# The low part of W1's chunks in the MLP loop: made by ScalarE and an accumulating GpSimd transfer instead of VectorE

## Chip, cores, metric

The kernel runs on one core of a Trainium2 chip. The metric is device time in microseconds (us) of one execution; a time is the median of several executions. Engines go by their short names in the rows: PE (TensorE, matmuls), PEld (its weight loads), DVE (VectorE), ACT (ScalarE), POOL (GpSimd), SP (SyncE, which issues the loads here).

## What is computed

One decoder layer on x of 256 tokens by 1024 in float32: a mixer of four column groups, and an MLP of width 4096. The change touches the MLP alone:

```python
for l in range(DEPTH):                      # DEPTH = 1
    h = rms_norm(x, pre_mix_g[l])
    u = h @ w_in[l]
    ...
    y = jnp.concatenate([y_a, y_b, y_c, y_d], axis=-1) @ w_out[l]
    x = x + rms_norm(y, post_mix_g[l])
    h = rms_norm(x, pre_mlp_g[l])
    m = jnp.square(jax.nn.relu(h @ mlp_w1[l])) @ mlp_w2[l]
    x = x + rms_norm(m, post_mlp_g[l])
```

## The kernel before

**Three products for one.** To keep float32 accuracy every large product is split. A weight chunk arrives as `raw` (128 partitions by 2048, 1 MB). ScalarE copies it to a tile `hi` of type fp32r (`split_hi`), VectorE writes `lo = raw - hi` (`split_lo`). The activations are split in the same way (`h2`, `h2L`; `mh`, `ml`). TensorE then runs three matmuls for each product: hi by hi, hi by activation lo, and lo by hi.

**The chunks.** `seq` (lines 87 to 92) lists all weight chunks in the order of use: 10 of W_in, 4 of W_out, then for the MLP `w1 0, w1 1, w2 0, w1 2, w2 1, w1 3, ...`, 16 of W1 and 16 of W2. Tiles come from the pool `wts`: four buffers each for `raw` and `hi`, three for `lo`, handed out in turn. So the `lo` of a chunk takes the buffer of the chunk that came three splits before it, and a `raw` that of the chunk four loads before it.

**The MLP loop** (lines 887 to 898) walks `seq` from n = 14. At a W1 chunk c it issues `up(c)`: 48 matmuls of 256 columns into a PSUM tile `pm`, in groups of three whose third reads `lo`. At a W2 chunk c it issues `down(c)`: 30 matmuls into the sums `acd` that stay in PSUM. After either, it issues the load of the chunk four places on (SP), the split of the chunk two places on, and after `up(c)` the squared ReLU and its split (`relu2`, `act`). Each engine works through its own instructions strictly in the program's order (`InOrder`), so PE runs up(1), down(0), up(2), down(1), up(3), ... without choice, and ACT runs for each c: relu of up(c), `mh` of c, `hi` of W2's chunk c, `hi` of W1's chunk c + 2. W1's chunks 0 and 1 are split ahead of the loop; the loop itself splits W1's chunks 2 to 15 and all of W2.

**The end.** `down(14)` and `down(15)` are ordered so that the first 128 tokens finish early; `finish` scales, adds the residual and stores the output in five pieces (SP). After that, lines 957 to 964 run 20 matmuls into a PSUM tile `shapes` which nothing reads.

In the profile all instructions carry the line of the helper (L60), so they are told apart by the names of their tiles: `hi_w`, `lo_w`, `raw_w` are the tiles of W1 and W2 alike.

Of the kernel before, what the change touches and what calls it, by code (L numbers as in the profile page):

```python
# [16 lines left out]
F32 = mybir.dt.float32  # L17
F32R = mybir.dt.float32r
BF16 = mybir.dt.bfloat16
AF = mybir.ActivationFunctionType  # L20
ALU = mybir.AluOpType
# [3 lines left out]
P = 128  # L25
# [3 lines left out]
NW = 2048  # L29
# [36 lines left out]
def hybrid_layer(ctx, tc, x, head, win, wout, w1, w2, gates, rows, out):  # L66
    nc = tc.nc
    V, A, G, T, Q = (InOrder(tc, e) for e in (nc.vector, nc.scalar, nc.gpsimd, nc.tensor, nc.sync))

    cst = ctx.enter_context(tc.tile_pool(name="cst", bufs=1))  # L70
    wts = ctx.enter_context(tc.tile_pool(name="wts", bufs=4))
# [11 lines left out]
    def mm(name):  # L83
        return pmm.tile([P, 512], F32, tag="mm", name=name)


    seq = [("in", c) for c in (0, 1, 8, 5, 6, 7, 9, 3, 4, 2)]
# [5 lines left out]
    src = {"in": win, "out": wout, "w1": w1, "w2": w2}  # L93
    raw, hi, lo = {}, {}, {}
# [6 lines left out]
    def load(n, parts=1):  # L101
        if n < len(seq):
            w, d = new_raw(n)
            for i in range(parts):
                c = slice(i * NW // parts, (i + 1) * NW // parts)
                Q.dma_start(w[:, c], d[:, c])
# [4 lines left out]
    def split_hi(n, i=0, parts=1):  # L111
        if n < len(seq):
            k = seq[n]
            if i == 0:
                hi[k] = wts.tile([P, NW], F32R, tag="hi", name=f"hi_{k[0]}{k[1]}")
            c = part(i, parts)
            A.activation(hi[k][:, c], raw[k][:, c], AF.Copy)

    def split_lo(n, i=0, parts=1):
        if n < len(seq):  # L120
            k = seq[n]
            if i == 0:
                lo[k] = wts.tile([P, NW], F32R, tag="lo", name=f"lo_{k[0]}{k[1]}", bufs=3)
            c = part(i, parts)
            V.tensor_tensor(lo[k][:, c], raw[k][:, c], hi[k][:, c].bitcast(F32), op=ALU.subtract)

    def split(n, parts=1):
        for i in range(parts):
            split_hi(n, i, parts)
            split_lo(n, i, parts)  # L130
# [6 lines left out]
    for blocks in HEAD:  # L137
        n = HOFF[blocks[-1]] + S
# [16 lines left out]
    warm = cst.tile([P, 256], BF16, name="warm")  # L155
# [117 lines left out]
    identb = cst.tile([P, P], BF16, name="identb")  # L273
# [568 lines left out]
    def up(c, between=None):  # L842
        pu = mm(f"pm{c}")
        H, L = hi["w1", c], lo["w1", c]
        for j in range(2):
            if j and between:
                between()
            o = pu[:, j * S:(j + 1) * S]
            for k in range(KT):
                ws = slice(k * S + j * P, k * S + (j + 1) * P)  # L850
                T.matmul(o, H[:, ws], h2[:, k, :], start=(k == 0), stop=False)
                T.matmul(o, H[:, ws], h2L[:, k, :], start=False, stop=False)
                T.matmul(o, L[:, ws], h2[:, k, :], start=False, stop=(k == KT - 1))
        return pu

    def relu2(pu):
        m = wk.tile([P, 512], F32, name="mr")
        A.activation(m, pu, AF.Relu)
        V.tensor_tensor(m, m, m, op=ALU.mult)
        return m  # L860

    def act(c, m):
        mh[c] = wk.tile([P, 512], F32R, name="mh", bufs=3)
        ml[c] = wk.tile([P, 512], F32R, name="ml", bufs=3)
        A.activation(mh[c], m, AF.Copy)
        V.tensor_tensor(ml[c], m, mh[c].bitcast(F32), op=ALU.subtract)

    m0 = relu2(pz[0])

    def act0():  # L870
# [12 lines left out]
    def down(c, t, h):  # L883
        wide("w2", c, lambda k, t: mh[c][:, k * S + t * P:k * S + (t + 1) * P],
             lambda k, t: ml[c][:, k * S + t * P:k * S + (t + 1) * P], t, accs[t, h], cols[t, h], c == 0, c == 15)

    for n in range(14, len(seq)):
        name, c = seq[n]
        if name == "w1":
            pm_ = up(c, act0 if c == 1 else None) if c else None  # L890
        elif c < 14:
            for t, h in sorted(cols):
                down(c, t, h)
        load(n + 4)
        split(n + 2)
        if pm_ is not None:
            act(c, relu2(pm_))
            pm_ = None
        if n == 14:

            for t in range(2):
                scr = few.tile([P, D], BF16, name="scr", bufs=1)
                ss = few.tile([P, 1], F32, name="ss")
                A.activation(scr, x1[t], AF.Square, accum_out=ss)
                V.tensor_scalar(q2[t], ss, 1.0 / D, RMS_EPS, op0=ALU.mult, op1=ALU.add)
                V.reciprocal(q2[t], q2[t])
# [47 lines left out]
    finish(1, ((0, 384), (384, 768), (768, 1024)))  # L954


    pb = mm("shapes")
    H15 = hi["w2", 15]
    wide_zeros = warm[:, None, :].to_broadcast([P, 2, 256])
    for lhs, rhs, n in ((H15[:, :P], H15[:, 512:1024], 512), (identb, wide_zeros, 512), (H15[:, :P], H15[:, 512:896], 384),  # L960
                        (H15[:, :P], H15[:, 512:576], 64)):
        for _ in range(5):
            T.matmul(pb[:, :n] if rhs is not wide_zeros else pb.rearrange("p (a b) -> p a b", a=2), lhs, rhs,
                     start=True, stop=True)


# [41 lines left out]
```

## Time and profile before

| | us |
|---|---|
| median of 3 runs (287.37 to 287.67) | 287.59 |
| the profiled execution | 288.29 |
| its span in the profile | 286.6 |
| PE busy / DVE / ACT / POOL | 279.3 / 193.6 / 152.6 / 22.3 |
| mean granted TensorE clock | 1.00 of full speed |

The profiled execution is 0.70 us above the median, and 1.69 us of it lie outside the span. Times inside the span are counted from its start. The MLP loop's PE work begins at 107.71 us with up(1) and is over at 279.60 us.

### The profile page before, as it was taken

The numbers are of one execution on the slowest core, as the hardware profiler recorded it, in microseconds if no ns is written. First come the engines' busy times: TensorE is split into PE (matmuls) and PEld (weight loads), VectorE is DVE, ScalarE is ACT, GpSimd is POOL, SyncE is SP. The second block draws the span as 40 slices with busy tenths as digits, with TensorE's granted clock in tenths as the row PEclk, the third lists the DMA queues.
The fourth block names the chain that finished last, engine by engine and source line by source line (L and its number), as shares of the span: only waits on it lengthen the run. The fifth ranks groups of instructions, "written<-read, shape, count | busy, mean of one in ns | idle before, by whom it ended". The sixth has DMA issues, their size and how long they took to land.

```text
span 286.6 us, 4726 instructions
## 1 busy us (share of the span) xinstructions
PE 279.3 (97%) x1954; PEld 255.9 (89%) x1954; DVE 193.6 (68%) x262; ACT 152.6 (53%) x192; POOL 22.3 (8%) x53
## 2 busy tenths in 40 slices
PE   6799999999999999999999999999999999999995
PEld 4699997999977899989999899899899899899883
DVE  1999999899989996765636646546447357257262
ACT  3995459875548849642632623624615515526141
POOL 4388500000000000000000000000000000000000
PEclk9999999999999999999999999999999999999999
DMA  6999446926404544675374383472472562600012
GB/s 210 412 409 334 150 156 225 411 74 238 146 2 153 213 150 173 266 287 214 101 281 166 129 293 133 165 293 96 199 287 74 226 255 69 266 0 0 2 73 74
DMA packets 9237, 53.04 MB, mean 185 GB/s; under 512 B 1024, under 2 KB 1536, under 8 KB 3712
## 3 DMA queue, kind: packets, MB, share of 16 engines
q1 hardware_dynamic: 9216, 52.75, 49.1%
q8 instruction: 15, 0.25, 0.3%
q14 instruction: 6, 0.05, 0.1%
HBM read 51.70 MB, written 1.05 MB: 184 GB/s over the span
## 4 chain that ended last, share of the span: by engine, by line
PE 94%; DMA 2%; DVE 1%; SPq 0%; ACT 0%; issue 0%
PE acd L60 31%; PE pm L60 29%; PE pu L60 19%; PE acc L60 7%; DMA hd<-in_head_dram 2%; PE pz L60 2%; PE shapes L60 1%; PE psc L60 1%; PE po L60 1%; DVE sq L60 1%; PE pg L60 1%; PE pth L60 0%; PE ptp L60 0%; SPq L60 0%; PE pvar L60 0%; DVE hF L60 0%
## 5 line engine op out<-in xcount | busy, mean ns | idle before, releaser
L60 DVE TENSOR_TENSOR lo_w<-raw_w,hi_w 128x2048 fp32r<-128x2048 f32 (+2 forms) x36 | 72.6, 2050 | 17.8 <-ACT hi_w L60 17.8
L60 PE MATMUL pm<-h2L,hi_w 128*128 128x256 f32 x240 | 66.5, 277 | 0.0
L60 PE MATMUL pm<-h2T,hi_w 128*128 128x256 f32 x240 | 66.5, 277 | 0.0
L60 PE MATMUL pm<-h2T,lo_w 128*128 128x256 f32 x240 | 66.4, 277 | 0.0
L60 ACT ACTIVATE hi_w<-raw_w 128x2048 fp32r<-128x2048 f32 (+1 forms) x33 | 59.6, 1849 | 1.3 <-issue 1.3
L60 PE MATMUL acd<-hi_w,ml 128*128 128x512 f32 (+1 forms) x160 | 56.0, 350 | 0.0
L60 PE MATMUL acd<-lo_w,mh 128*128 128x512 f32 (+1 forms) x160 | 55.8, 349 | 0.0
L60 PE MATMUL acd<-hi_w,mh 128*128 128x512 f32 (+1 forms) x160 | 55.8, 348 | 0.0
L60 ACT ACTIVATE mr<-pm 128x512 f32<-128x512 f32 x15 | 8.9, 596 | 73.8 <-PE pm L60 73.8
L60 PEld LDWEIGHTS pm<-h2T,hi_w 128*128 128x128 f32 x240 | 45.1, 188 | 0.0
L60 PEld LDWEIGHTS pm<-h2T,lo_w 128*128 128x128 f32 x240 | 45.1, 188 | 0.0
L60 PEld LDWEIGHTS pm<-h2L,hi_w 128*128 128x128 f32 x240 | 45.1, 188 | 0.0
L60 DVE TENSOR_TENSOR mr<-mr 128x512 f32<-128x512 f32 x16 | 11.1, 693 | 44.7 <-ACT mr L60 44.7
L60 PE MATMUL pu<-hT,hi_in 128*128 128x256 f32 x128 | 36.3, 284 | 0.0
L60 PE MATMUL pu<-hT,lo_in 128*128 128x256 f32 x128 | 35.9, 280 | 0.0
L60 PE MATMUL pu<-hL,hi_in 128*128 128x256 f32 x128 | 35.9, 280 | 0.0
L60 PEld LDWEIGHTS acd<-lo_w,mh 128*128 128x128 f32 x160 | 30.2, 189 | 4.2
L60 PEld LDWEIGHTS acd<-hi_w,ml 128*128 128x128 f32 x160 | 30.1, 188 | 4.2
L60 PEld LDWEIGHTS acd<-hi_w,mh 128*128 128x128 f32 x160 | 30.1, 188 | 4.1
L60 DVE SCALAR_TENSOR_TENSOR cacc<-zpad,prm,cacc 128x256 f32<-128x256 f32 x60 | 25.3, 477 | 0.1
L60 PEld LDWEIGHTS pu<-hT,hi_in 128*128 128x128 f32 x128 | 24.3, 190 | 0.0
L60 PEld LDWEIGHTS pu<-hT,lo_in 128*128 128x128 f32 x128 | 24.2, 189 | 0.0
(177 smaller groups left out, 381.3 us busy)
## 6 DMA issues: line engine op xcount, KB each, us to landing
raw_w<-in_w_dram SPq DMA_DIRECT2D x32, 1024.0 KB, 4.9
raw_in<-in_win_dram SPq DMA_DIRECT2D x7, 1024.0 KB, 5.6
raw_out<-in_wout_dram SPq DMA_DIRECT2D x4, 1024.0 KB, 4.9
raw_in<-in_win_dram SPq DMA_DIRECT2D x4, 512.0 KB, 7.9
hd<-in_head_dram SPq DMA_DIRECT2D x3, 384.0 KB, 5.9
x<-in_x_dram SPq DMA_DIRECT2D x2, 512.0 KB, 7.5
grow<-in_rows_dram SPq DMA_DIRECT2D x2, 512.0 KB, 7.1
hd<-in_head_dram SPq DMA_DIRECT2D x2, 256.0 KB, 4.9
```

The lines of the kernel that those rows point to most:

```text
L60: ins = f(*args, **kwargs)
```

## The change

For W1's chunks 2 to 15 the loop no longer calls `split` but `split_dma`: ScalarE writes `hi` as before, then a second ScalarE instruction writes `-hi` to the `lo` tile, and GpSimd issues a transfer that reads the chunk from HBM once more and adds it to what stands in the `lo` tile. W2's chunks are split as before. The 20 matmuls into `shapes` are gone.

```diff
+    def split_dma(n):
+
+        k = seq[n]
+        split_hi(n)
+        lo[k] = wts.tile([P, NW], F32R, tag="lo", name=f"lo_{k[0]}{k[1]}", bufs=3)
+        A.activation(lo[k], hi[k].bitcast(F32), AF.Copy, scale=-1.0)
+        G.dma_start(lo[k], src[k[0]][k[1]], accum_op=ALU.add)
...
-        split(n + 2)
+        if n + 2 < len(seq) and seq[n + 2][0] == "w1":
+            split_dma(n + 2)
+        else:
+            split(n + 2)
...
-    pb = mm("shapes")
-    H15 = hi["w2", 15]
-    wide_zeros = warm[:, None, :].to_broadcast([P, 2, 256])
-    for lhs, rhs, n in ((H15[:, :P], H15[:, 512:1024], 512), (identb, wide_zeros, 512), (H15[:, :P], H15[:, 512:896], 384),
-                        (H15[:, :P], H15[:, 512:576], 64)):
-        for _ in range(5):
-            T.matmul(pb[:, :n] if rhs is not wide_zeros else pb.rearrange("p (a b) -> p a b", a=2), lhs, rhs,
-                     start=True, stop=True)
```

What it moves on the engines shows best at the start of the loop. First ACT, from the first split inside the loop on: `hi_w_1393` is the `hi` of W1's chunk 2 and `lo_w_1395` its `lo`, `mr` and `mh` belong to the squared ReLU of up(1), and the last two `hi_w` are W2's chunk 1 and W1's chunk 3.

```order
 L60 ACTIVATE mh<-ptm 128x512
 L60 ACTIVATE hi_w_1393<-raw_w_1301 128x2048
+L60 ACTIVATE lo_w_1395<-hi_w_1393 128x2048
 L60 ACTIVATE mr<-pm_1332 128x512
 L60 ACTIVATE mh<-mr 128x512
-L60 ACTIVATE hi_w_1436<-raw_w_1316 128x2048
-L60 ACTIVATE hi_w_1491<-raw_w_1391 128x2048
-L60 ACTIVATE mr<-pm_1440 128x512
```

One ACT instruction of a whole chunk has come in ahead of the squared ReLU of up(1), and one stands at the same place in each later turn of the loop. Next DVE at the same place: `lo_w_1438` is W2's chunk 1 and `lo_w_1493` W1's chunk 3.

```order
 L60 TENSOR_TENSOR ml<-ptm,mh 128x512
-L60 TENSOR_TENSOR lo_w_1395<-raw_w_1301,hi_w_1393 128x2048
 L60 TENSOR_TENSOR mr<-mr 128x512
 L60 TENSOR_TENSOR ml<-mr,mh 128x512
-L60 TENSOR_TENSOR lo_w_1438<-raw_w_1316,hi_w_1436 128x2048
-L60 TENSOR_TENSOR lo_w_1493<-raw_w_1391,hi_w_1491 128x2048
+L60 TENSOR_TENSOR lo_w_1439<-raw_w_1316,hi_w_1437 128x2048
```

DVE loses the subtraction of every W1 chunk from 2 on and keeps those of W2 (the same tile is 1438 in one build and 1439 in the other). Last GpSimd, whose instructions ended before with the four `alibi` tiles of the mixer:

```order
 L60 TENSOR_SCALAR alibi<-dist 128x256 x4
-L1004 UNCONDITIONAL_BRANCH
-L1004 ISA
+L60 DMA lo_w_1395<-in_w_dram 128x2048
+L60 DMA lo_w_1494<-in_w_dram 128x2048
+L60 DMA lo_w_1593<-in_w_dram 128x2048
```

Fourteen such transfers follow one another there; nothing else is added to this engine.

## Rows read from the trace of the kernel before

**Rows 1.** The page, parts 1 and 2: busy time; the span in 40 slices, tenths.

```profile
PE 279.3 (97%) x1954; PEld 255.9 (89%) x1954; DVE 193.6 (68%) x262; ACT 152.6 (53%) x192; POOL 22.3 (8%) x53
...
PE   6799999999999999999999999999999999999995
...
PEclk9999999999999999999999999999999999999999
```

**Rows 2.** The page, part 4: shares of the chain that ended last, by engine.

```profile
PE 94%; DMA 2%; DVE 1%; SPq 0%; ACT 0%; issue 0%
```

**Rows 3.** That chain in order of time: start us, us, what.

```profile
107.71 2.83 PE pm L60 x24
...
113.72 5.59 PE acd L60 x30
119.31 5.45 PE pm L60 x48
124.76 5.59 PE acd L60 x30
...
207.68 5.45 PE pm L60 x48
213.13 5.59 PE acd L60 x30
218.73 5.46 PE pm L60 x48
...
279.60 3.61 PE shapes L60 x20
```

**Rows 4.** ACT in order of time, start of the loop: start, us, instructions.

```profile
112.80 1.91 ACT L60 ACTIVATE hi_w<-raw_w 128x2048 fp32r<-128x2048 f32 x1
114.60 0.58 ACT L60 ACTIVATE mr<-pm 128x512 f32<-128x512 f32 x1
117.67 0.63 ACT L60 ACTIVATE mh<-mr 128x512 fp32r<-128x512 f32 x1 [2.48 <-DVE mr L60]
118.20 3.71 ACT L60 ACTIVATE hi_w<-raw_w 128x2048 fp32r<-128x2048 f32 x2
```

**Rows 5.** PE in order of time, first lo product of up(2).

```profile
119.14 0.28 PE L60 MATMUL pm<-h2T,hi_w 128*128 128x256 f32 x1
...
119.38 0.28 PE L60 MATMUL pm<-h2T,lo_w 128*128 128x256 f32 x1
```

**Rows 6.** ACT in order of time, one later turn of the loop.

```profile
204.08 3.70 ACT L60 ACTIVATE hi_w<-raw_w 128x2048 fp32r<-128x2048 f32 x2
```

**Rows 7.** DVE in order of time, the same turn.

```profile
206.01 4.49 DVE L60 TENSOR_TENSOR lo_w<-raw_w,hi_w 128x2048 fp32r<-128x2048 f32 x2 [1.11 <-ACT hi_w L60]
```

**Rows 8.** SP in order of time, the first load that turn frees.

```profile
208.33 13.57 SPq L60 DMA_DIRECT2D raw_w<-in_w_dram  x4
```

**Rows 9.** Stretches of that turn: busy of each engine, clock, DMA share, GB/s.

```profile
204.00:209.00 5.00, 5.00 (x35) 4.59 (x34) 3.68 (x3) 3.79 (x3) 0.00 (x0) 1.00 0.00 0
209.00:215.00 6.00, 6.00 (x46) 5.65 (x45) 2.20 (x2) 1.01 (x2) 0.00 (x0) 1.00 0.91 345
215.00:216.00 1.00, 1.00 (x6) 0.78 (x6) 0.69 (x1) 1.00 (x2) 0.00 (x0) 1.00 0.08 33
```

**Rows 10.** Issues and landings of W1's and W2's loads.

```profile
DMA to landing us min/median/max: 4.7/4.9/6.5
```

**Rows 11.** Groups of instructions from 130 to 260 us, DVE and ACT chunk instructions.

```profile
L60 DVE TENSOR_TENSOR lo_w<-raw_w,hi_w 128x2048 fp32r<-128x2048 f32 x24 | 53.9, 2288 | 13.3 <-ACT hi_w L60 13.3
...
L60 ACT ACTIVATE hi_w<-raw_w 128x2048 fp32r<-128x2048 f32 x24 | 44.5, 1900 | 0.0
```

**Rows 12.** SP in order of time, the last output stores.

```profile
281.53 1.35 SPq L60 DMA_DIRECT2D out_dram<-u  x3
```

**Rows 13.** DMA issues: KB each, median us to landing (the last output piece).

```profile
out_dram<-u SPq DMA_DIRECT2D x1, 128.0 KB, 2.9
```

**Rows 14.** Waits, SP: us in total, times, longest (the program's end).

```profile
SPq L1004 <- PEq L1004: 1.0, 2, 0.8
```

## Prediction

> **What bounds the kernel now.** I read the page first: PE is busy 97% of the span, its slices stand at nine tenths from the third to the last but one, and the granted clock is at its upper level (2.4 GHz) in all of them [rows 1]. The chain that ended last is 94% PE [rows 2]. In order of time it has no piece of another engine in the MLP loop: down(0) starts at 113.72, up(2) at 119.31 when it ends, down(1) at 124.76, and a late turn (207.68, 213.13, 218.73) has the same spacing; a turn of up and down takes 5.45 + 5.59 = 11.04 us [rows 3]. So VectorE and ScalarE work there for nothing but being in time, and what the change does to the end is decided by one question: is the low part of a W1 chunk ready when its up() begins? For that I read when ScalarE finishes `hi` [rows 4, 6], when PE first reads a `lo` [rows 5], and what the DMA engines do in between [rows 8 to 10].
>
> **What goes.** Fourteen subtractions of 2.29 us [rows 11], 32 us of VectorE. None lies on the chain, so they are worth 0. The 20 unread matmuls take 3.61 us from 279.60 and end at 283.21 [rows 3], but the output's last store is issued between 281.53 and 282.88 [rows 12] and takes 2.9 us to land [rows 13], until 285.4 or so; they are covered by it: 0. At most it is the 0.8 us that SP's longest wait for PE in the closing lines took [rows 14]; the other end is 0, and I take 0, because the store outlasts them by 2 us.
>
> **What comes on ScalarE.** Fourteen more passes over a chunk. Two passes in a row take 3.71 us [rows 4], so one more is 1.80. A turn's ScalarE work is about 0.58 + 0.63 + 3.70 us [rows 4, 6] and becomes 6.7 of 11.04: 0. At the loop's start the pass delays the relu of up(1) from 114.60 to about 116.4, but in the kernel before `mh` there waited 2.48 us for VectorE's square, until 117.67 [rows 4], and the subtraction ahead of that square is gone; `mh` stays near its place: 0.
>
> **The accumulating transfer.** No row shows one. Call D the time from the end of ScalarE's `-hi` to the chunk's landing.
> - *Lower bound:* a plain 1 MB load, 4.9 us from issue to landing, 4.7 to 6.5 [rows 10].
> - *What a plain load consists of:* in a turn the DMA engines are idle from 204 to 209, then share 0.91 over six microseconds and 0.08 over one [rows 9]: 6 x 0.91 + 0.08 = 5.54 us for two chunks, so 2.77 us of moving for 1 MB. The remaining 4.9 - 2.77 = 2.13 us is the way in and out.
> - *My value:* an add needs both operands, the chunk from HBM and the 1 MB that already stands in `lo`: two chunks' reading, 5.54 us. For GpSimd's part I add its mean instruction, 22.3 us over 53 = 0.42 us [rows 1]. D alone = 0.42 + 2.13 + 5.54 = 8.1 us.
> - *Upper bound:* the nearest row for a slower adder is none; I take four chunks' moving, 0.42 + 2.13 + 11.1 = 13.6.
>
> The Trainium skill (Collectives: The Full Stack, The bandwidth ceiling: the fold count and why AG ≠ RS ≠ AR) says that a transfer that adds is not slowed by the arithmetic but by reading two sources, and gives a ratio of 1.93 against a copy. By it the moving would be 2.77 x 1.93 = 5.3 us, an estimate; by the row alone, read as a price for one chunk whatever is done with it, 2.77. No run here shows such a transfer.
>
> **The first one, W1's chunk 2.** ScalarE starts its `hi` at 112.80; two passes later `-hi` is there, 112.80 + 3.71 = 116.51 [rows 4]. PE reads the first `lo` of up(2) at 119.38, only two matmuls after up(2) began [rows 5]. The cover is 2.87 us. The loads that ran with it are a single chunk in flight at most, so D alone holds: PE waits 8.1 - 2.9 = **5.2 us**. By the lower bound it is 4.9 - 2.9 = 2.0, by the upper 10.7. Behind the waiting matmul is all of PE's queue, and every other engine waits for PE. This stall is inside the program order and can't be worked around.
>
> **The second, chunk 3.** ScalarE is not held by PE yet: its two `hi` begin at 118.20 [rows 4], and with `-hi` it is done at 118.20 + 3.71 + 1.80 = 123.7. up(3) started at 124.76 + 5.59 = 130.35 [rows 3] and now comes 5.2 later: cover 11.8, more than any D below. 0.
>
> **The turns after that, chunks 4 to 15.** `-hi` needs a `lo` buffer, which is free only when down(c - 1) has ended, 207.68 in the turn I read; ScalarE's two `hi` end at 204.08 + 3.70 = 207.78 [rows 6], `-hi` at 209.58. up(c + 2) begins at 218.73 [rows 3] and reads `lo` 0.07 later: cover 9.2 us. D alone, 8.1, would fit. But the same moment frees two `raw` buffers: W2's when VectorE's first subtraction of the turn ends (206.01 and 4.49 for two, so 208.3 [rows 7]), and SP issues at 208.33 [rows 8]; W1's now already with ScalarE's `hi` at 207.78, so its load no longer waits for a second subtraction and follows at once. GpSimd issues at 209.58 + 0.42 = 210.0, 1.67 us behind them, with 5.54 - 1.67 = 3.9 us of their moving still to do. Served ahead of the loads it lands after 8.1 us (no stall), behind them after 8.1 + 3.9 = 12.0 (stall 2.8). I take packet against packet, the adding one counting two: two thirds of the engines' time, 5.54 x 1.5 = 8.31, D = 0.42 + 2.13 + 8.31 = 10.9, a stall of 10.9 - 9.2 = 1.65 us in each turn. A stall moves everything alike, so it comes again next turn. Chunks 4 to 14 meet two loads (the last three loads fall to chunks 13 and 14), chunk 15 none: 11 x 1.65 = **18.0 us**, bounds 0 and 11 x 2.8 = 31.
>
> **Sum.** 5.2 + 0 + 18.0 = 23.2 on the profiled execution's 288.29 us: 311.5. That execution stood 0.70 above the median of the runs, so against the median 287.59 I forecast **310.8 us**.
>
> **The rivals.**
> 1. *Only the first stall remains*: the transfer wins against the loads, or costs little more than a plain one. For it: D alone fits under 9.2, and the DMA engines are idle more than half of a turn [rows 9]. Against: the loads are issued 1.67 us earlier. 287.6 + 2.0 to 5.2 = 289.7 to 292.8.
> 2. *The adder is slower than two reads.* With three chunks' moving, 8.31: alone D = 10.9, first stall 8.0; beside loads three quarters of the time, 11.1, D = 13.6, stall 4.4 in 11 turns = 48.5, and 1.7 for chunk 15. Sum 58, 346 us; with four chunks' about 382. Nothing in the trace speaks for or against.
> 3. *The clock falls.* PE has no long wait in this trace, and the clock never left 2.4 GHz [rows 1]; a wait of 5 us is new. At 1.2 GHz up(2) alone would take 5.45 more: 316. The Trainium skill (TensorE: Matmul & The Clock Gate, HAM oscillation — how this bites in real kernels) says that waits for transfers between groups of matmuls can put the array back to half its clock, and that it then starts cold. No stretch of this trace shows it.
> 4. *Not slower.* It needs the first chunk landed within 2.87 us of `-hi`, and every later one within 9.2. Then PE never waits, the time is 287.6, or 286.8 with the 0.8 us of the closing wait. For it there is only that a transfer's own moving can be 2.77 us; against it, that no 1 MB load in the loop landed in under 4.7 [rows 10]. That the change doesn't do what it says is not at issue: each listed transfer is there on GpSimd.
>
> **How the numbers follow.** Forecast 0.36, only the first stall 0.27, slower adder 0.24, clock 0.08, not slower 0.05. The forecast's own range, by the share that the loads take, is 287.6 + 5.2 = 292.8 to 287.6 + 5.2 + 31 = 323.8. For 8 in 10 I leave out not slower (0.05) and the upper half of the slower adder (0.12): 289.7 to 346. A measurement of this kernel can tell about 0.2% (0.6 us) from no change. Slower by more than that are all cases but the last: 0.95; of the last I give 0.03 to within 0.2% and 0.02 to faster.
>
> **What would show it.** In the profile after: 14 adding transfers whose landing can be read; a wait of PE for `lo_w` before up(2) of about 5 us, none before up(3), then some 1.6 us before each up() to chunk 14 and none at chunk 15; up and down otherwise 5.45 and 5.59; VectorE's `lo_w` 14 fewer; the end from the last `acd` to the span's end unchanged. Wrong would be: no wait at up(2) (rival 4), waits at up(2) alone (rival 1), waits of 4 us and more in each turn (rival 2), or up() itself longer at a granted clock under 1.00 (rival 3).

## The result and the profile after

The changed kernel takes **312.76 us** (median of 4 runs, 312.05 to 315.59) against 287.60 for the kernel before on the same chip: ratio 1.0895, 95% interval 1.0824 to 1.0965. The forecast was 310.8 us, with a range of 289.7 to 346. The execution that was profiled is the longest of the four, 315.59 us with a span of 313.9; the span has grown by 27.3 us where the median has grown by 25.2. In two of the experiments below (4 and 7) the profile is of an execution that the comparisons leave out, so only a single place is read from it.

The page of the changed kernel, parts 1 to 3, answers to [rows 1]: PE is down to 90% of the span, its slices dip all through the loop, and the granted clock has dips too. DMA share has risen to nearly ten tenths there; the new queue q0 carries GpSimd's transfers.

```profile
PE 282.6 (90%) x1934; PEld 257.6 (82%) x1934; DVE 162.7 (52%) x248; ACT 179.6 (57%) x206; POOL 34.6 (11%) x67
...
PE   6899999999999991899799699889978999799992
...
PEclk9999999999999996699899999979999999999998
DMA  7997539363053589919987996994998989957003
...
q0 software_dynamic: 2016, 14.68, 23.4%
```

VectorE's busy time fell by 193.6 - 162.7 = 31 us and bought nothing, as foreseen. The waits view of the changed kernel (who waits for whom, us in total, times, longest) names what PE had never waited for before:

```profile
PEld pm L60 <- DMA lo_w<-in_w_dram: 23.8, 10, 8.6
PE pm L60 <- DMA lo_w<-in_w_dram: 21.8, 9, 8.4
```

In order of time these are PE's first matmuls on a landed `lo` (start, us, instruction, idle time before it and its releaser). The chunks are 2, 4, 6, 8, 10, 11, 12, 13 and 14; chunks 3, 5 and 9 have no wait, chunk 7 one of 0.2 us that only PE's weight loads show, chunk 15 none:

```profile
126.93 0.58 PE L60 MATMUL pm<-h2T,lo_w 128*128 128x256 f32 x1 [8.42 <-DMA lo_w<-in_w_dram]
153.15 0.39 PE L60 MATMUL pm<-h2T,lo_w 128*128 128x256 f32 x1 [2.11 <-DMA lo_w<-in_w_dram]
179.86 0.38 PE L60 MATMUL pm<-h2T,lo_w 128*128 128x256 f32 x1 [2.71 <-DMA lo_w<-in_w_dram]
204.88 0.39 PE L60 MATMUL pm<-h2T,lo_w 128*128 128x256 f32 x1 [2.40 <-DMA lo_w<-in_w_dram]
230.86 0.39 PE L60 MATMUL pm<-h2T,lo_w 128*128 128x256 f32 x1 [1.96 <-DMA lo_w<-in_w_dram]
243.41 0.38 PE L60 MATMUL pm<-h2T,lo_w 128*128 128x256 f32 x1 [1.22 <-DMA lo_w<-in_w_dram]
255.26 0.38 PE L60 MATMUL pm<-h2T,lo_w 128*128 128x256 f32 x1 [0.53 <-DMA lo_w<-in_w_dram]
268.37 0.39 PE L60 MATMUL pm<-h2T,lo_w 128*128 128x256 f32 x1 [1.78 <-DMA lo_w<-in_w_dram]
280.40 0.39 PE L60 MATMUL pm<-h2T,lo_w 128*128 128x256 f32 x1 [0.70 <-DMA lo_w<-in_w_dram]
```

The first is 8.4 us, the others add up to 13.4. The transfers themselves, issues with KB each and median us to landing, then all landings of `lo_w`, then three of GpSimd's issues in order of time (the first, that of chunk 4, and the last, of chunk 15):

```profile
raw_w<-in_w_dram SPq DMA_DIRECT2D x32, 1024.0 KB, 6.1
lo_w<-in_w_dram POOLq DMA_DIRECT2D x14, 1024.0 KB, 11.6
...
DMA to landing us min/median/max: 7.9/11.6/13.2
...
115.94 1.04 POOL L60 DMA_DIRECT2D lo_w<-in_w_dram  x1 [83.28 <-ACT lo_w L60]
142.05 0.86 POOL L60 DMA_DIRECT2D lo_w<-in_w_dram  x1 [17.84 <-ACT lo_w L60]
281.74 0.86 POOL L60 DMA_DIRECT2D lo_w<-in_w_dram  x1 [12.24 <-ACT lo_w L60]
```

The reader should see two things. The last transfer, the only one without a load beside it, is the one that lands in 7.9 us; the median is 11.6. And from the issue of chunk 4 to that of chunk 15 there are 11 turns in 139.7 us, 12.7 each against 11.04 [rows 3].

The clock is the third item. Stretches of the changed kernel (columns as in [rows 9]: PE busy with its matmuls, PEld, DVE, ACT, POOL, granted clock, DMA share, GB/s), around the waits before up(2), up(4) and up(6), and after that before up(8):

```profile
120.00:122.00 2.00, 0.00 (x0) 0.00 (x0) 1.62 (x1) 1.97 (x2) 0.00 (x0) 0.61 1.02 205
122.00:126.00 4.00, 0.00 (x0) 0.00 (x0) 0.00 (x0) 1.03 (x1) 0.87 (x1) 0.50 0.99 295
126.00:130.00 4.00, 3.07 (x14) 3.07 (x15) 0.00 (x0) 0.00 (x0) 0.00 (x0) 0.50 1.02 320
130.00:132.00 2.00, 2.00 (x17) 2.00 (x16) 0.00 (x0) 0.00 (x0) 0.00 (x0) 0.83 0.96 262
151.00:153.00 2.00, 0.04 (x1) 0.00 (x0) 0.38 (x1) 1.79 (x1) 0.00 (x0) 1.00 0.88 188
153.00:156.00 3.00, 2.85 (x19) 2.85 (x20) 0.00 (x0) 0.00 (x0) 0.86 (x1) 0.76 0.99 374
156.00:158.00 2.00, 2.00 (x11) 2.00 (x11) 0.00 (x0) 0.00 (x0) 0.00 (x0) 0.50 1.06 324
...
178.00:180.00 2.00, 0.14 (x1) 0.14 (x2) 0.00 (x0) 0.90 (x1) 0.81 (x1) 1.00 0.84 246
180.00:182.00 2.00, 2.00 (x18) 2.00 (x19) 0.00 (x0) 0.00 (x0) 0.05 (x1) 1.00 1.04 381
...
206.00:209.00 3.00, 3.00 (x16) 3.00 (x15) 0.00 (x0) 0.00 (x0) 0.00 (x0) 0.50 1.04 344
```

The clock is at half (1.2 GHz) for the rest of the first wait and the first 3.6 us of up(2), once more after the wait before up(4), not after that before up(6), and again at up(8).

**Where the 27.3 us are.** The chain of the changed kernel, in order of time, ends its loop with `down(14)` and `down(15)`; the two lines before that show up() after a wait and at full clock, and up(2) at half clock:

```profile
126.93 7.26 PE pm L60 x46
...
280.40 5.51 PE pm L60 x46
...
296.95 11.23 PE acd L60 x60
```

From up(2)'s first matmul to the last `acd` PE took 308.18 - 118.11 = 190.1 us, before it took 279.60 - 119.14 = 160.5 [rows 3, 5]: 29.6 more. The listed waits are 8.4 + 13.4 = 21.8 of it. The half clock costs 7.26 - 5.51 = 1.75 us in up(2), and about 1.6 each in up(4) and up(8), which take 7.0 us from the end of the wait to the first matmul of down() where up(14) takes 5.34; 5.0 in all. The other 2.8 are the ends of the ten waits, 0.27 or so each: a wait is counted from the modelled end of the matmul before it, 0.28 us after its start, while matmuls that follow each other start 0.12 apart, and the first matmul after a wait holds the next one up by another 0.1. Against these 29.6 stand 1.0 us by which up(2) comes earlier than before (118.11 against 119.14, in code that the change does not touch) and 1.3 us of a shorter end, whose last store lands in 1.9 us instead of 2.9 [rows 13]. The missing matmuls don't account for the shorter end: in experiment 1, which leaves out only them, the store takes 2.9 us and the end 7.0, as before.

The two shortest of the four executions (312.05 and 312.14 us) have a mean clock of 0.987 and 0.985 and are 3.5 us shorter than the profiled one, about what its two later falls cost (3.3). That those two executions had only the first fall is likely, but no profile of them shows it.

### The profile page after: what moved, and what is told of

The parts are those of the page before. It is cut to its first block, busy times and chain, and to the rows that moved or that the text cites. A ratio compares the mean times of both kernels' runs of the same rounds, so it can differ in the third digit from the quotient of the medians.

```text
span 313.9 us, 4692 instructions
## 1 busy us (share of the span) xinstructions
PE 282.6 (90%) x1934; PEld 257.6 (82%) x1934; DVE 162.7 (52%) x248; ACT 179.6 (57%) x206; POOL 34.6 (11%) x67
## 4 chain that ended last, share of the span: by engine, by line
issue 41%; PE 41%; DMA 9%; POOL 3%; ACT 2%; DVE 2%; SPq 0%; DVEq 0%; POOLq 0%; ACTq 0%
PE pu L60 17%; DMA lo_w<-in_w_dram 7%; PE acc L60 7%; PE pm L60 6%; PE acd L60 5%; POOL lo_w L60 3%; DMA hd<-in_head_dram 2%; PE pz L60 2%; ACT hi_w L60 1%; PE psc L60 1%; PE po L60 1%; DVE sq L60 1%; ACT lo_w L60 1%; PE pg L60 1%; DVE u L60 0%
## 5 line engine op out<-in xcount | busy, mean ns | idle before, releaser
L60 PE MATMUL pm<-h2T,lo_w 128*128 128x256 f32 x240 | 69.9, 291 | 21.8 <-DMA lo_w<-in_w_dram 21.8
L60 PE MATMUL pm<-h2T,hi_w 128*128 128x256 f32 x240 | 68.7, 286 | 0.0
L60 PE MATMUL pm<-h2L,hi_w 128*128 128x256 f32 x240 | 68.6, 286 | 0.0
L60 PEld LDWEIGHTS pm<-h2T,lo_w 128*128 128x128 f32 x240 | 47.4, 197 | 23.8 <-DMA lo_w<-in_w_dram 23.8
L60 DVE TENSOR_TENSOR mr<-mr 128x512 f32<-128x512 f32 x16 | 11.1, 694 | 106.2 <-ACT mr L60 106.2
L60 DVE TENSOR_TENSOR lo_w<-raw_w,hi_w 128x2048 fp32r<-128x2048 f32 (+2 forms) x22 | 41.7, 1902 | 16.7 <-ACT hi_w L60 16.7
L60 PEld LDWEIGHTS pm<-h2T,hi_w 128*128 128x128 f32 x240 | 47.5, 198 | 0.0
L60 PEld LDWEIGHTS pm<-h2L,hi_w 128*128 128x128 f32 x240 | 47.4, 197 | 0.0
L60 POOL DMA_DIRECT2D lo_w<-in_w_dram x14 | 12.3, 875 | 237.7 <-ACT lo_w L60 237.7
L60 ACT ACTIVATE lo_w<-hi_w 128x2048 fp32r<-128x2048 f32 x14 | 26.8, 1914 | 0.4
## 6 DMA issues: line engine op xcount, KB each, us to landing
lo_w<-in_w_dram POOLq DMA_DIRECT2D x14, 1024.0 KB, 11.6
```

Of the source, the lines that this page charges most:

```text
L60: ins = f(*args, **kwargs)
```

## The experiments

The kernel before had a median of 287.74 us beside these runs. Ratios are against it.

**1. Only the unread matmuls gone.** The kernel before without lines 957 to 964.

```diff
-    pb = mm("shapes")
...
-            T.matmul(pb[:, :n] if rhs is not wide_zeros else pb.rearrange("p (a b) -> p a b", a=2), lhs, rhs,
-                     start=True, stop=True)
```

> The kernel before without its 20 unread matmuls, and nothing else of the change. Theory: they lie beside the last output store, so the time stays at 287.6 within 0.3. Rival: the closing wait of SP for PE (0.8 us in the kernel before) is theirs, and the time falls to about 286.8.

287.67 us against 287.74; ratio 0.9989, interval 0.9969 to 1.0008. Nothing that can be told from no change. That part of the change is worth 0 as far as this can tell; the rival's 0.8 us is just inside the interval's lower end (0.9 us), but the medians differ by 0.1, and the profile speaks against it: SP's longest closing wait for PE is 0.8 us there too, without the matmuls.

**2. Does the add make the transfer long, or GpSimd's issue?** The same 14 transfers as plain copies.

```diff
-        G.dma_start(lo[k], src[k[0]][k[1]], accum_op=ALU.add)
+        G.dma_start(lo[k], src[k[0]][k[1]])
```

> The changed kernel with the same 14 GpSimd transfers as plain copies, without the add; the low part then holds the whole chunk, so the second product of W1 is not the one that is wanted. Theory (the add moves two chunks' bytes): moving 2.8 us less alone and 5.5 beside the loads, landing 5 us after issue alone and 7 to 8 beside loads, under the cover of 9.2, so no waits in later turns and 3 to 5.5 us before up(2); 290 to 295. Rival (it is GpSimd's way of issuing that is slow, not the add): landings stay at 11 us and the time at 312.

294.70 us; ratio 1.0238 (1.0203 to 1.0272). In its profile PE's matmuls wait once, before up(2), and nowhere else in the loop; only its weight loads wait 0.3 us more in a later turn (PE in order of time, then the issues and the landings of `lo_w`):

```profile
124.33 0.58 PE L60 MATMUL pm<-h2T,lo_w 128*128 128x256 f32 x1 [5.10 <-DMA lo_w<-in_w_dram]
...
lo_w<-in_w_dram POOLq DMA_DIRECT2D x14, 1024.0 KB, 7.7
...
DMA to landing us min/median/max: 5.1/7.7/9.1
```

Alone (the shortest, again the last) a plain copy lands in 5.1 us and an adding one in 7.9. The difference, 2.8 us, is one more chunk's moving, 2.77 by [rows 9]. The stretches of these two lone transfers show it directly: the adding one keeps the DMA engines at a share of 0.83 for 7 us (283 to 290 us of the changed kernel), 5.8 us of moving, and the plain one at 0.58 for 5 us (263 to 268 us here), 2.9. So the add occupies the engines twice as long, and the issue by GpSimd is not what is slow: 5.1 against 4.9 for SP's loads [rows 10]. The moving goes from 2.77 to 2.77 + 2.8 = 5.57 us, a ratio of 2.0. The Trainium skill's ratio between a step that adds and one that copies, which it measured in collectives (Collectives: The Full Stack, The bandwidth ceiling: the fold count and why AG ≠ RS ≠ AR), is 1.93; the trace agrees.

**3. Half the transfers.** Odd chunks split by VectorE, even ones as changed.

```diff
-        if n + 2 < len(seq) and seq[n + 2][0] == "w1":
+        if n + 2 < len(seq) and seq[n + 2][0] == "w1" and seq[n + 2][1] % 2 == 0:
```

> The changed kernel with only W1's even chunks (2, 4, ... 14) by the adding transfer, the odd ones by VectorE: half the transfers. Theory (PE's wait before one up() is cover for the next chunk, so two neighbours share one deficit of about 2.1 to 2.7 us): waits of 1.8 to 2.7 us before up(4), up(6) ... up(14), 11 to 16 in all, about as much as the changed kernel's 13.4 with twice the transfers; wait before up(2) as there; time 309 to 313. Rival (every transfer costs alike, 13.4 over 12, 1.1 us): 6 x 1.1 = 6.7 us, time 304 to 306.

316.34 us; ratio 1.1001 (1.0967 to 1.1035): half the transfers, and no less time; it is 3 us above the theory's 309 to 313. PE's waits in its profile (chunks 2, 4, ... 14):

```profile
127.94 0.58 PE L60 MATMUL pm<-h2T,lo_w 128*128 128x256 f32 x1 [8.70 <-DMA lo_w<-in_w_dram]
154.38 0.38 PE L60 MATMUL pm<-h2T,lo_w 128*128 128x256 f32 x1 [1.87 <-DMA lo_w<-in_w_dram]
179.33 0.39 PE L60 MATMUL pm<-h2T,lo_w 128*128 128x256 f32 x1 [2.58 <-DMA lo_w<-in_w_dram]
206.06 0.39 PE L60 MATMUL pm<-h2T,lo_w 128*128 128x256 f32 x1 [2.75 <-DMA lo_w<-in_w_dram]
230.62 0.38 PE L60 MATMUL pm<-h2T,lo_w 128*128 128x256 f32 x1 [1.99 <-DMA lo_w<-in_w_dram]
256.27 0.39 PE L60 MATMUL pm<-h2T,lo_w 128*128 128x256 f32 x1 [1.66 <-DMA lo_w<-in_w_dram]
281.04 0.39 PE L60 MATMUL pm<-h2T,lo_w 128*128 128x256 f32 x1 [2.40 <-DMA lo_w<-in_w_dram]
```

The six later ones add up to 13.25 us, where the changed kernel's later ones add up to 13.4 with twice as many transfers. That settles the rule: `-hi` of chunk c + 2 is written when down(c - 1) ends, and what PE then waits before up(c + 1) is cover for chunk c + 2 as well. Two neighbours share one deficit, landing plus issue less 9.2 us; it doesn't come in each turn. That this kernel's median is even above the changed one's is the clock's doing as far as the profiles tell. The two profiled executions differ by only 0.8 us (316.40 and 315.59), with 22.0 and 21.8 us of waits. But this kernel's mean granted clock was 0.971 to 0.972 in all four runs, the changed kernel's 0.969, 0.975, 0.985 and 0.987, the lower the longer.

**4. The first transfer one chunk later.** Chunk 2 by VectorE, chunk 3 the first adding one.

```diff
-        if n + 2 < len(seq) and seq[n + 2][0] == "w1":
+        if n + 2 < len(seq) and seq[n + 2][0] == "w1" and seq[n + 2][1] > 2:
```

> The changed kernel with W1's chunk 2 split by VectorE again, so that chunk 3 has the first adding transfer. Theory (a stall is D less the cover, and the cover counts what PE waits in between): the wait of 8.4 us before up(2) goes, but chunk 3 loses the 8.4 us that it had on top of its own cover of 6.7, so with D of 11 to 11.6 PE waits 4.3 to 4.9 us before up(3); later turns as in the changed kernel; time some 4 to 6 below it, 307 to 309. Rival (the 8.4 us is a price of the first transfer as such, GpSimd after a long rest): PE waits 8 us and more before up(3), time unchanged at about 313. Second rival (the wait belongs to chunk 2 alone): no wait before up(3), about 302.5.

Ratio 1.0710 (1.0656 to 1.0764), about 308 us (two executions, 306.7 and 309.3). Of its profile only the wait before up(3) is read: 5.7 us, 0.8 above the range of the theory. The miss is the landing: 12.0 us after the issue, where the theory had 11 to 11.6 in all; 12.0 + 0.3 - 6.7 is 5.6. Both rivals fall: it is neither 8.4 again nor nothing. The wait follows the cover of the chunk that happens to be first.

**5. The loads behind the add.** GpSimd issues the loop's loads itself, after the adding transfer of the turn; only the first two (18 and 19 of `seq`) stay with SP.

```diff
-        load(n + 4)
...
+        if n == 14:
+            load(18)
+            load(19)
+        elif name == "w1":
+            load(n + 5, eng=G)
+            load(n + 6, eng=G)
```

(`load` takes the engine as an argument; the two `load` calls of a turn stand after the split.)

> The changed kernel with the loop's loads from the chunk 20 of the sequence on issued by GpSimd behind the adding transfer of the same turn, instead of by SP ahead of it; same bytes, same 14 adds. Theory (the later turns' waits are the time that the loads take ahead of the add): the add lands about 8 us after issue, as the last one did alone (7.9), under the cover of 9.2, so no waits in later turns beyond 0.3; before up(2) PE waits 5 to 6 us instead of 8.4, because that transfer too met loads; one fall of the clock there (2 to 3 us); time 294 to 297. Rival (the DMA engines are full whatever the order, 5.5 + 5.5 us of moving in a turn of 11.04): waits stay at 1 us and more in each turn and the time above 302.

296.60 us; ratio 1.0331 (1.0294 to 1.0367). Same bytes, same 14 adds, 16 us less. Its profile has one wait, and the median landing is that of the lone transfer (PE in order of time; issues; the landings; then the stretch from 150 to 250 us, and last the same stretch of the changed kernel):

```profile
125.49 0.58 PE L60 MATMUL pm<-h2T,lo_w 128*128 128x256 f32 x1 [5.61 <-DMA lo_w<-in_w_dram]
...
lo_w<-in_w_dram POOLq DMA_DIRECT2D x14, 1024.0 KB, 7.9
...
DMA to landing us min/median/max: 7.9/7.9/11.9
...
150.00:250.00 100.00, 99.99 (x706) 92.70 (x705) 33.29 (x28) 61.03 (x46) 17.58 (x27) 1.00 0.97 285
...
150.00:250.00 100.00, 89.60 (x607) 82.67 (x607) 27.55 (x23) 50.62 (x38) 6.90 (x8) 0.97 0.89 248
```

PE is busy for 99.99 of 100 us while the DMA engines stand at 0.97; in the changed kernel the same stretch has a share of 0.89 with PE at 89.6, in the kernel before 0.51. So it was not the amount of transfers but their order: loads that nobody needed for a turn went ahead of the one that PE was about to need. The experiment changes two things, the order and the engine that issues the loads, but one of its own transfers tells them apart: chunk 3's add, issued at 124.59 us, still met the two loads that GpSimd had issued from 117.97 on, and it landed only after 11.9 us. With loads ahead of it in GpSimd's own queue it was as late as behind SP's (median 11.6 in the changed kernel). Before up(2) PE waits 5.6 us, and its weight loads wait 0.2 us in one later turn.

**6. The same, starting at chunk 4.**

```diff
-        if n + 2 < len(seq) and seq[n + 2][0] == "w1":
+        if n + 2 < len(seq) and seq[n + 2][0] == "w1" and seq[n + 2][1] > 3:
```

> The same, and chunks 2 and 3, whose own cover is 2.9 and 6.7 us, split by VectorE; 12 adds left. Theory: no wait of PE anywhere in the loop, clock at its upper level throughout, time within 1 us of the kernel before, 287.3 to 288.7. Rival as above: 300 and more.

287.92 us against 287.74; ratio 1.0012 (0.9987 to 1.0038): the whole loss is gone with 12 adding transfers left. Three small waits that the theory left out remain in its profile, 0.35, 0.40 and 0.55 us. A likely reason, not tested, is that two chunks' loads and a doubled one are to be moved in a turn that has just room for them (5.54 + 5.57 = 11.1 of 11.04 us). It doesn't beat the kernel before: VectorE's time was free there, and PE's is the same in both.

**7. PE kept busy in the first wait.**

```diff
+            if c == 2:
+                pf = mm("fill")
+                for _ in range(FILL):
+                    T.matmul(pf[:, :256], warm[:, :P], warm, start=True, stop=True)
             pm_ = up(c, act0 if c == 1 else None) if c else None
```

> The changed kernel with 75 matmuls of 256 columns (bf16, zeros, 0.11 us each, 8.2 us in all) that nothing reads between down(0) and up(2), where PE waits 8.4 us. Theory (the wait's length is the transfer's; part of the loss is the clock that falls in it): up(2) starts to read lo at the same time as in the changed kernel, the clock stays at its upper level from 118 to 132 us, and up(2)'s 46 matmuls after the wait take 5.2 us instead of 7.26, so 2 us less at that place; later falls of the clock as before. Time 309 to 312. Rival (the matmuls add to the wait): 8 us more, 320.

310.23 us; ratio 1.0780 (1.0748 to 1.0811), 2.5 us below the changed kernel's 312.76. Only the time around up(2) is read from its profile, from its chain and its stretches:

```profile
118.42 8.21 PE fill L61 x75
126.62 5.67 PE pm L61 x48
...
122.00:124.00 2.00, 2.00 (x21) 1.80 (x19) 0.00 (x0) 1.18 (x1) 0.51 (x1) 1.00 0.98 201
126.00:128.00 2.00, 2.00 (x20) 1.96 (x19) 0.00 (x0) 0.00 (x0) 0.00 (x0) 1.00 0.94 324
```

The clock stays at 2.4 GHz, and fill and up(2) together take 13.9 us where the changed kernel's up(2) with its wait takes 118.11 to 134.01, 15.9 us. Work that is thrown away made the kernel 2 us faster at that place: the idle time there had a price beyond its length, and 1.75 us of it was the clock.

## Why the prediction was right, and where it was wrong

- *What bounds the kernel, and that a transfer lands too late for it:* right. PE's waits for `lo_w` make the loss.
- *What goes is worth 0:* right, for VectorE's 31 us and the unread matmuls (experiment 1).
- *ScalarE's passes cost 0:* right. No wait of PE for ScalarE in the MLP loop stands in the waits view.
- *D alone, 8.1 us:* right. 7.9 from issue, and 0.3 from the end of `-hi` to the issue (141.76 to 142.05 for chunk 4), so 8.2.
- *The first stall, 5.2 us:* wrong by 3.2. The step that failed is "The loads that ran with it are a single chunk in flight at most, so D alone holds". It reads the loads of the kernel before, where the next one was issued only at 117.05 us, when VectorE's subtraction had freed its buffer, and so after the 116.51 at which it has `-hi` ready. In the changed kernel `hi` alone frees it, as the prediction itself says of the later turns, and SP issued that load at 113.69, 2.25 us ahead of the add (115.94); two more followed at 121.12 and 121.65, while the add was still moving. The landing took 10.9 us. With those loads issued behind it (experiment 5) it took 8.2, and PE's wait was 5.6.
- *The second, chunk 3, nothing:* right.
- *The turns after that, 11 x 1.65 = 18.0:* the sum held better than its parts; the waits were 13.4. Two steps failed in opposite directions. D beside the loads was taken as 10.9, and the landings' median of 11.6 with 0.3 ahead of it gives 11.9. And "A stall moves everything alike, so it comes again next turn" is false: a wait before one up() is cover for the next chunk (experiment 3). With the rule put right and D as measured, a pair of turns shares 11.9 - 9.2 = 2.7 us, 1.35 a turn.
- *The end unchanged:* wrong by 1.3 us; it became shorter, and the cause stays open.
- *The clock falls (rival 3, 0.08):* it did, beside the forecast and not in place of it. It cost 5.0 us in the profiled execution. At up(2) alone it was 1.75, not 5.45, since the clock was back after 3.6 us of work. The Trainium skill's rule that waits for transfers can put the array back to half its clock (TensorE: Matmul & The Clock Gate, HAM oscillation — how this bites in real kernels) is borne out by the stretches around up(2), which resumes at half; before up(4) the clock was still at full when PE resumed, and after the wait before up(6) it stayed there.

So the total of 310.8 is near the 312.8 measured in part because a first stall that was too small and a fallen clock that was left out stood against later stalls that were too large. That part of the agreement is luck. The mechanism is shown by experiments 2, 3, 5 and 6; the sizes of its terms were not all right.

## What to carry to other kernels

Here a transfer that adds into SBUF occupied the DMA engines as long as two plain ones. Count it so until a trace of your own says otherwise, and look at what else is queued at the moment when it is issued: a load whose buffer comes free at the same time and which is not needed for a turn belongs behind it. An engine with idle time is no reason to relieve it if its result was in time; moving its work to a path of 8 to 12 us needs cover of that length at every use, the first one above all. Stalls in a pipelined loop are not to be multiplied by the turns before it is clear whether one stall lengthens the cover of the next.

## What was not expected of the hardware

The clock also fell after waits of 2.1 and 2.4 us (up(4), up(8)), and there only when PE was at work again: 1.00 up to 153 us, at half from 156 to 158, though PE went on at 153.15; after a wait of 2.7 us before up(6) it didn't fall. How often it falls differs between executions of the same kernel (mean clock 0.969 to 0.987), and the longest of the four runs is the one with the lowest. Where the adding transfers run, the DMA engines at a share of 1.02 moved 205 GB/s (120 to 122 us); the last one, alone, shows 213 GB/s at 1.02 (287 to 288 us), half of the 426 at 1.07 of experiment 2's lone plain copy (265 to 266 us). A low rate beside a full share is how such a transfer looks in the stretches.
